# Seven products for 28 of the 32 hidden blocks of an MLP, and a last stage that goes token tile by token tile

## The chip, the cores and the metric

The kernel runs on one core of one Trainium2 chip. The metric is device time in microseconds for one execution of the whole decoder layer; several executions of a kernel are timed, one more is recorded by the profiler.

## The reference

One decoder layer on 512 tokens of width 1024, in float32. A token mixer (gated linear attention and latent attention, merged by gates) and an MLP each end in a residual sum and a layer norm:

```python
h = layer_norm(x, ln_in_g, ln_in_b)
...
mix = token_mixer(h, cos, sin, w_in[l], w_gla_a2[l], ...)
h = layer_norm(DEEPNORM_ALPHA * h + mix, ln1_g[l], ln1_b[l])
ff = jnp.square(jax.nn.relu(h @ w_ff1[l])) @ w_ff2[l]
h = layer_norm(DEEPNORM_ALPHA * h + ff, ln2_g[l], ln2_b[l])
```

The part that counts here is `ff`: `h` is 512 x 1024, `w_ff1` 1024 x 4096, `w_ff2` 4096 x 1024. The hidden width of 4096 is 32 blocks of 128.

## The kernel before

**Precision.** Every float32 operand of a large matmul is split into a high part (rounded to the matmul's format, on ACT) and a low part (the rest, on DVE): `split` at L104 for activations, L180 and L181 for weights. A product is then three matmuls: high x high, low x high, high x low.

**Weights.** `plan` appends the weight items to one list, `stream`, in the order in which the matmuls will use them. `pump(i)` (L152) runs ahead of item `i`: it issues loads on SP's queue into three `wraw` buffers, and splits the items that come next into `whi`/`wlo` (two buffers each), or into buffers of the general pool of 24 (`home` "a"), or back into `wraw` ("r"). Items whose source is already in SBUF carry `src` and `home` and no load.

**The MLP.** The loop over `ci` takes the hidden width in four chunks of eight blocks. In each, `gemm_fm` (L231 to L233) computes the first product with the hidden units on the partitions, and `ev_h` takes each block out of PSUM: relu, then square.

For chunks 0 to 2 the second product uses a scheme of seven products for a 2 x 2 by 2 x 2 block product (Winograd's form of Strassen's). The tokens are halved (0 to 255, 256 to 511), the hidden blocks are paired, the columns of `w_ff2` are halved. `win_hid` forms the sums of the hidden operand (tile `hx`), `win_sums` and a line of `win_f2` those of the weight quarters (tiles `T1`, `T2`, and in place T3 and T4); the quarters are loaded by `win_load` on POOL's queue (L1061). The table `WIN` gives the order: (weight operand, half of the chunk's blocks, product number). `win_f2` runs the products (L1116 to L1118), each in two PSUM banks of 128 tokens x 512 columns; some products add to the bank of an earlier one. When the second half of a product is done, ACT copies the bank to a buffer `ev` (L1128), and POOL issues DMAs that add it to the residual tiles `res` in SBUF (L1130), one DMA for each residual tile half that the product belongs to.

For chunk 3 the second product is an ordinary one: `ev_h` makes high and low parts of each hidden block (the square for the low part on POOL, L1159), and `gemm_tm` (L264 to L266) takes token tiles 0 and 1 together over all eight blocks, then tile 2; a loop written out (L1191 to L1193) takes tile 3, its second half in two strips of 256 columns, each with its own statistics. A tile's result is added to `res` on DVE (`ev_res`, L992, and L1195). `ln2` then aggregates the statistics, takes the power -1/2 on POOL (L1047), centres and scales on DVE (L1050, L1051) and writes the halves out on SP's queue (L1052).

**Order.** The program is traced in Python; a scheduler then sets a fixed order of instructions for each engine, by program order and a simulated time, and allots buffers. So an instruction whose operands are ready may stand ahead of earlier lines. Each engine and each queue then runs strictly in that order. PSUM has eight banks: four in the pool of `MM()`, four in that of `PX()`. The pool `pb` has 22 buffers (for `relu`, `ev`, and others), tag "C" has eight (four residual tiles, `T1`, `T2`, and the rows of gain and shift, `bc`).

Of the kernel before, what the change touches and what calls it, by code (L numbers as in the profile page):

```python
# [52 lines left out]
def tile_hybrid_block(ctx: ExitStack, tc: tile.TileContext, I, out, dbg=None):  # L53
# [259 lines left out]
    def plan_zip(key, specs):  # L313
        pls = [{"idx": [], "nk": 8, "per": 2} for _ in specs]
        for k0 in range(0, 8, 2):
# [12 lines left out]
           ("T4", 0, 4), ("T4", 1, 4), ("22", 0, 5), ("22", 1, 5), ("T3", 0, 6), ("T3", 1, 6))  # L328
    fb = 0
    for ci in range(FC):  # L330
        nb = 8
        for b, w in F1[ci]:
            PL["f1", ci, b] = plan("w_ff1", (fb + b) * P, w * P, res=(ci == 0 and b == 0), per=8 // w)
        if ci < FC - 1:
            PL["f2", ci] = []
            for n, (op, hf, _) in enumerate(WIN):
                PL["f2", ci].append(len(stream))
                stream.append({"src": lambda q=(ci, op, hf): WQ[q], "nk": 2, "n": T, "res": False,
                               "ahead": 2, "home": HOMES[n]})
        else:  # L340
            plan_zip("f2last", [("w_ff2", 0, fb, True), ("w_ff2", T, fb, True)])
        fb += nb
# [695 lines left out]
    def ln2(tt, bst=None):  # L1038
        mv = S([P, 2], F32, "mv")
        r = res[tt]  # L1040
        if bst is None:
            bst = S([P, 2, 6], F32, "bst")
            for j in range(2):
                nc.vector.bn_stats(bst[:, j, :], r[:, j * T:(j + 1) * T])
        nc.vector.bn_aggr(mv, bst)
        vts(mv[:, 1:2], mv[:, 1:2], LN_EPS, None, op0=ALU.add)
        gtt(mv[:, 1:2], mv[:, 1:2], mhalf[:, 0:1], op=ALU.pow)  # L1047
        for j in range(2):
            c = slice(j * T, (j + 1) * T)
            stt(r[:, c], r[:, c], mv[:, 0:1], bg[:, c], op0=ALU.subtract, op1=ALU.mult)  # L1050
            stt(r[:, c], r[:, c], mv[:, 1:2], bb[:, c], op0=ALU.mult, op1=ALU.add)  # L1051
            nc.sync.dma_start(out[tt * P:(tt + 1) * P, c], r[:, c])  # L1052
        yield

    def win_load(ci):
        w2 = I["w_ff2"].rearrange("(k p) n -> p k n", p=P)
        for op, i, j in (("12", 0, 1), ("11", 0, 0), ("22", 1, 1), ("21", 1, 0)):
            for hf in range(2):
# [5 lines left out]
    def win_sums(ci):  # L1064
# [5 lines left out]
        for hf in range(2):  # L1070
# [29 lines left out]
    def win_f2(ci, hid):  # L1100
        bank = {}
        for n, (op, hf, ph) in enumerate(WIN):
            i = PL["f2", ci][n]
            pump(i)
            hi, lo = stream[i]["w"]
            for pp in range(2):
                for t in range(2):
# [10 lines left out]
                    mm(o, xl[:, c], hi[:, pp], start=False, stop=hf == 1 and pp == 1, skip_group_check=True)  # L1118
                tick(4)
            if n in (5, 6):  # L1120
                t2, q21 = WT.pop((ci, n - 5))
                vtt(t2, t2, q21, op=ALU.subtract)
                WQ[ci, "T4", n - 5] = t2
            if hf == 1:
# [122 lines left out]
```

## Time and profile before

| | us |
|---|---|
| median of 3 runs | 903.77 |
| lowest, highest | 902.82, 903.8 |
| the profiled execution | 902.75 |
| its span, first to last instruction | 901.0 |

| busy, share of span | |
|---|---|
| PE (matmul) | 98% |
| DVE | 61% |
| ACT | 46% |
| POOL | 19% |

The profile is one execution recorded by hardware. In its rows L12 is line 12 of the kernel, `out<-in` names the tiles with their buffer numbers left out, `x16` is a count, and the time in brackets is idle time before an instruction with what ended it. PE is TensorE, PEld its weight loads, DVE VectorE, ACT ScalarE, POOL GpSimd, SP the engine whose queue issues most loads. A name with q (POOLq) is an engine's sequencer. A matmul's listed duration overlaps the next one's; from start to start is what it costs.

### The profile page before, as it was taken

What the parts mean: (1) busy time and instruction counts of PE and PEld (TensorE: products, weight loads), DVE (VectorE), ACT (ScalarE), POOL (GpSimd) and SP (SyncE); (2) the same over time, 40 slices, a digit from 0 to 9 for tenths busy, and PEclk for the clock granted to TensorE, in tenths of its full rate; (3) what the DMA queues carried; (4) which work ended last, traced back from release to release, by engine and by line L of the source; (5) the groups of instructions that cost most, each with busy time, mean ns of one, the idle gap of its engine ahead of it and who ended that gap; (6) DMA issues with size and microseconds to landing.
All of it is one profiled execution on the core that took longest, in us unless ns stands there. A gap on an engine that the chain in (4) does not pass through costs nothing.

```text
span 901.0 us, 11740 instructions
## 1 busy us (share of the span) xinstructions
PE 883.8 (98%) x4508; PEld 751.3 (83%) x4508; DVE 553.4 (61%) x905; ACT 412.7 (46%) x701; POOL 170.1 (19%) x192
## 2 busy tenths in 40 slices
PE   6999999999999999999999999999999999999996
PEld 5988888888888888888888888988888888888886
DVE  7835855575635244657756797997557646723576
ACT  6455443444434333435645423366357546643410
POOL 1003442442511010000000002104400520141201
PEclk9999999999999999999999999999999999999999
DMA  7413313212212332212207618005950990494312
GB/s 244 121 47 94 91 51 94 71 47 71 76 38 92 88 105 70 72 41 66 94 24 258 210 47 303 2 0 138 301 121 25 265 247 25 107 213 104 126 69 83
DMA packets 61159, 97.80 MB, mean 109 GB/s; under 512 B 7552, under 2 KB 27392, under 8 KB 61104
## 3 DMA queue, kind: packets, MB, share of 16 engines
q1 hardware_dynamic: 48816, 68.23, 23.9%
q0 software_dynamic: 10368, 25.17, 11.6%
q10 hardware_dynamic: 1920, 3.66, 1.2%
q8 instruction: 35, 0.57, 0.3%
q14 instruction: 20, 0.16, 0.1%
HBM read 82.36 MB, written 2.10 MB: 94 GB/s over the span
## 4 chain that ended last, share of the span: by engine, by line
PE 97%; ACT 1%; POOL 1%; DVE 1%; DMA 1%; issue 0%; SPq 0%; DVEq 0%
PE mm L231 16%; PE mm L233 15%; PE mm L232 15%; PE mm L264 7%; PE mm L266 7%; PE mm L265 7%; PE px L1116 2%; PE px L1118 2%; PE px L1117 2%; PE mm L1116 2%; PE mm L1118 2%; PE mm L1117 2%; PE px L679 2%; PE px L836 1%; PE px L366 1%; PE px L264 1%
## 5 line engine op out<-in xcount | busy, mean ns | idle before, releaser
L181 DVE TENSOR_TENSOR wlo<-wraw,whi 128x1024 fp32r<-128x1024 f32 (+1 forms) x104 | 117.7, 1133 | 169.6 <-ACT whi L180 162.2
L231 PE MATMUL mm<-h,whi 128*128 128x512 f32 x416 | 162.6, 392 | 0.4 <-ACT gt L923 0.4
L232 PE MATMUL mm<-h,whi 128*128 128x512 f32 x416 | 162.3, 390 | 0.0
L180 ACT ACTIVATE whi<-wraw 128x1024 fp32r<-128x1024 f32 (+1 forms) x104 | 100.3, 964 | 134.1 <-PE mm L232 82.4
L233 PE MATMUL mm<-h,wlo 128*128 128x512 f32 x416 | 154.4, 390 | 0.0
L231 PEld LDWEIGHTS mm<-h,whi 128*128 128x128 f32 x416 | 78.1, 188 | 16.3 <-ACT gt L923 0.6
L233 PEld LDWEIGHTS mm<-h,wlo 128*128 128x128 f32 x416 | 77.9, 188 | 16.4 <-DVE wlo L181 0.3
L232 PEld LDWEIGHTS mm<-h,whi 128*128 128x128 f32 x416 | 78.1, 188 | 15.7
L1130 POOL DMA_DIRECT2D res<-ev x48 | 42.2, 1042 | 188.9 <-ACT ev L1128 151.5
L265 PE MATMUL mm<-wlo,h 128*128 128x512 f32 x128 | 50.3, 393 | 0.0
L266 PE MATMUL mm<-whi,h 128*128 128x512 f32 x128 | 50.1, 392 | 0.0
L264 PE MATMUL mm<-whi,h 128*128 128x512 f32 x128 | 49.7, 403 | 0.0
L351 POOL TENSOR_TENSOR mv<-mv,mhalf 128x1 f32<-128x1 f32 x4 | 4.6, 1155 | 211.5 <-DVE mv L350 211.5
L180 ACT ACTIVATE xh<-wraw 128x1024 fp32r<-128x1024 f32 (+1 forms) x28 | 27.3, 986 | 34.8 <-PE mm L266 16.1
L618 POOL TENSOR_TENSOR rp<-rp 128x256 f32<-128x256 f32 x32 | 31.5, 984 | 60.8 <-ACT E L623 44.0
L1144 ACT ACTIVATE relu<-mm 128x512 f32<-128x512 f32 x32 | 18.8, 596 | 50.7 <-PE mm L233 50.6
L625 DVE TENSOR_TENSOR M<-E,qk 128x512 f32<-128x512 f32 x32 | 27.3, 854 | 16.5 <-ACT E L623 16.5
L181 DVE TENSOR_TENSOR xl<-wraw,xh 128x1024 fp32r<-128x1024 f32 (+1 forms) x28 | 31.1, 1126 | 8.0 <-ACT xh L180 8.0
L623 ACT ACTIVATE E<-rp 128x512 f32<-128x512 f32 x32 | 20.4, 638 | 26.9 <-POOL rp L619 26.9
L619 POOL TENSOR_TENSOR rp<-rp 128x256 f32<-128x256 f32 x32 | 27.6, 862 | 10.3 <-ACT q L648 8.1
L266 PEld LDWEIGHTS mm<-whi,h 128*128 128x128 f32 x128 | 24.1, 188 | 5.0
L265 PEld LDWEIGHTS mm<-wlo,h 128*128 128x128 f32 x128 | 24.1, 188 | 4.3
(369 smaller groups left out, 2196.1 us busy)
## 6 DMA issues: line engine op xcount, KB each, us to landing
wraw<-in_w_in_dram SPq DMA_DIRECT2D x40, 512.0 KB, 3.5
wraw<-in_w_ff_dram SPq DMA_DIRECT2D x40, 512.0 KB, 4.5
wq<-in_w_ff_dram POOLq DMA_DIRECT2D x24, 512.0 KB, 8.8
res<-ev POOLq DMA_DIRECT2D x48, 256.0 KB, 6.6
wraw<-in_w_o_gla_dram SPq DMA_DIRECT2D x8, 512.0 KB, 3.7
wraw<-in_w_o_mla_dram SPq DMA_DIRECT2D x8, 512.0 KB, 3.2
wraw<-in_w_out_dram SPq DMA_DIRECT2D x8, 512.0 KB, 4.0
wraw<-in_w_in_dram SPq DMA_DIRECT2D x8, 360.0 KB, 5.1
```

Of the source, the lines that this page charges most:

```text
L180: st["ins"] = act(hi[:, :nk, :n], raw[:, :nk, :n], AF.Copy)
L181: vtt(lo[:, :nk, :n], raw[:, :nk, :n], f(hi[:, :nk, :n]), op=ALU.subtract)
L231: mm(o, hi[:, c], xh, start=first, stop=False)
L232: mm(o, hi[:, c], xl, start=False, stop=False)
L233: mm(o, lo[:, c], xh, start=False, stop=last)
L264: mm(o, xh, hi[:, :n], start=opens, stop=False, skip_group_check=share)
L265: mm(o, xh, lo[:, :n], start=False, stop=False, skip_group_check=share)
L266: mm(o, xl, hi[:, :n], start=False, stop=last, skip_group_check=share)
L1116: mm(o, xh[:, c], hi[:, pp], start=opens, stop=False, skip_group_check=True)
L1117: mm(o, xh[:, c], lo[:, pp], start=False, stop=False, skip_group_check=True)
L1118: mm(o, xl[:, c], hi[:, pp], start=False, stop=hf == 1 and pp == 1, skip_group_check=True)
L1130: nc.gpsimd.dma_start(res[tt + t][:, j * T:(j + 1) * T], e, accum_op=ALU.add)
```

## The change

Chunk 3 uses the seven-product scheme for its first four blocks (one half in place of two: `HALVES`, `win_items`), with weight quarters loaded by `win_load(3)` on POOL's queue during chunk 2. Its last four blocks are an ordinary product, taken token tile by token tile. For tiles 2 and 3 ACT first copies the residual into the PSUM bank, and the matmuls add to it without a start flag; no add on DVE follows, and statistics and normalisation read PSUM. For tiles 0 to 2 the shift row is written to the output beforehand on SP's queue, ACT normalises, DVE multiplies by the gain, and a DMA on POOL's queue adds the tile to the output. Tile 3 is written as before. The evacuations of the seven products, L1128 and L1130, now occur in chunk 3 too.

```diff
@@ -326,19 +326,24 @@
     HOME = {"w": ("whi", "wlo"), "r": ("wraw", "wraw"), "a": ("xh", "xl")}
     WIN = (("11", 0, 0), ("21", 0, 1), ("11", 1, 0), ("21", 1, 1), ("T1", 0, 2), ("T1", 1, 2), ("T2", 0, 3), ("T2", 1, 3),
            ("T4", 0, 4), ("T4", 1, 4), ("22", 0, 5), ("22", 1, 5), ("T3", 0, 6), ("T3", 1, 6))
+
+    HALVES = (2, 2, 2, 1)
+
+    def win_items(ci):
+        return WIN if HALVES[ci] == 2 else [WIN[n] for n in (0, 1, 4, 6, 10, 8, 12)]
+
     fb = 0
     for ci in range(FC):
         nb = 8
         for b, w in F1[ci]:
             PL["f1", ci, b] = plan("w_ff1", (fb + b) * P, w * P, res=(ci == 0 and b == 0), per=8 // w)
-        if ci < FC - 1:
-            PL["f2", ci] = []
-            for n, (op, hf, _) in enumerate(WIN):
-                PL["f2", ci].append(len(stream))
-                stream.append({"src": lambda q=(ci, op, hf): WQ[q], "nk": 2, "n": T, "res": False,
-                               "ahead": 2, "home": HOMES[n]})
-        else:
-            plan_zip("f2last", [("w_ff2", 0, fb, True), ("w_ff2", T, fb, True)])
+        PL["f2", ci] = []
+        for n, (op, hf, _) in enumerate(win_items(ci)):
+            PL["f2", ci].append(len(stream))
+            stream.append({"src": lambda q=(ci, op, hf): WQ[q], "nk": 2, "n": T, "res": False,
+                           "ahead": 2, "home": (HOMES if ci < FC - 1 else "wwawawa")[n]})
+        if ci == FC - 1:
+            PL["f2last"] = [plan("w_ff2", j * T, T, fb + 4, fb + 8, res=True) for j in range(2)]
         fb += nb
 
 
@@ -1035,27 +1040,34 @@
             yield
 
 
-    def ln2(tt, bst=None):
-        mv = S([P, 2], F32, "mv")
-        r = res[tt]
-        if bst is None:
-            bst = S([P, 2, 6], F32, "bst")
+    def ln2(tt, bst, src):
+        mv, r = S([P, 2], F32, "mv"), res[tt]
+        rows = out[tt * P:(tt + 1) * P, :]
+        mean, var = mv[:, 0:1], mv[:, 1:2]
+        nc.vector.bn_aggr(mv, bst)
+        vts(var, var, LN_EPS, None, op0=ALU.add)
+        gtt(var, var, mhalf[:, 0:1], op=ALU.pow)
+        if tt < 3:
+
+            nmr = S([P, 1], F32, "nmr")
+            stt(nmr, mean, -1.0, var, op0=ALU.mult, op1=ALU.mult)
+            for c, p in src if tt > 1 else ((slice(0, D), r),):
+                act(r[:, c], p, AF.Identity, scale=var, bias=nmr)
+                vtt(r[:, c], r[:, c], bg[:, c], op=ALU.mult)
+            nc.gpsimd.dma_start(rows, r, accum_op=ALU.add)
+        else:
+            for c, p in src:
+                stt(r[:, c], p, mean, bg[:, c], op0=ALU.subtract, op1=ALU.mult)
             for j in range(2):
-                nc.vector.bn_stats(bst[:, j, :], r[:, j * T:(j + 1) * T])
-        nc.vector.bn_aggr(mv, bst)
-        vts(mv[:, 1:2], mv[:, 1:2], LN_EPS, None, op0=ALU.add)
-        gtt(mv[:, 1:2], mv[:, 1:2], mhalf[:, 0:1], op=ALU.pow)
-        for j in range(2):
-            c = slice(j * T, (j + 1) * T)
-            stt(r[:, c], r[:, c], mv[:, 0:1], bg[:, c], op0=ALU.subtract, op1=ALU.mult)
-            stt(r[:, c], r[:, c], mv[:, 1:2], bb[:, c], op0=ALU.mult, op1=ALU.add)
-            nc.sync.dma_start(out[tt * P:(tt + 1) * P, c], r[:, c])
+                c = slice(j * T, (j + 1) * T)
+                stt(r[:, c], r[:, c], var, bb[:, c], op0=ALU.mult, op1=ALU.add)
+                nc.sync.dma_start(rows[:, c], r[:, c])
         yield
 
     def win_load(ci):
         w2 = I["w_ff2"].rearrange("(k p) n -> p k n", p=P)
         for op, i, j in (("12", 0, 1), ("11", 0, 0), ("22", 1, 1), ("21", 1, 0)):
-            for hf in range(2):
+            for hf in range(HALVES[ci]):
                 t = A([P, 2, T], F32, "wq")
                 k0 = 8 * ci + 4 * hf + i
                 nc.gpsimd.dma_start(t, w2[:, k0:k0 + 3:2, j * T:(j + 1) * T])
@@ -1067,7 +1079,7 @@
                 if "ev" in st:
                     gates.enter_context(tc.issue_after(st["ev"].ins))
                 vtt(*a, **kw)
-        for hf in range(2):
+        for hf in range(HALVES[ci]):
             q12 = WQ.pop((ci, "12", hf))
             t1 = WQ[ci, "T1", hf] = A([P, 2, T], F32, "T1")
             held(t1, q12, WQ[ci, "11", hf], op=ALU.subtract)
@@ -1099,9 +1111,10 @@
 
     def win_f2(ci, hid):
         bank = {}
-        for n, (op, hf, ph) in enumerate(WIN):
+        nh = HALVES[ci]
+        for n, (op, hf, ph) in enumerate(win_items(ci)):
             i = PL["f2", ci][n]
-            pump(i)
+            pump(i + max(0, n - 3) if nh == 1 else i)
             hi, lo = stream[i]["w"]
             for pp in range(2):
                 for t in range(2):
@@ -1115,34 +1128,35 @@
                     xh, xl = hid[2 * hf + pp][ph]
                     mm(o, xh[:, c], hi[:, pp], start=opens, stop=False, skip_group_check=True)
                     mm(o, xh[:, c], lo[:, pp], start=False, stop=False, skip_group_check=True)
-                    mm(o, xl[:, c], hi[:, pp], start=False, stop=hf == 1 and pp == 1, skip_group_check=True)
+                    mm(o, xl[:, c], hi[:, pp], start=False, stop=hf == nh - 1 and pp == 1, skip_group_check=True)
                 tick(4)
-            if n in (5, 6):
-                t2, q21 = WT.pop((ci, n - 5))
+            if n in ((5, 6) if nh == 2 else (2,)):
+                h = n - 5 if nh == 2 else 0
+                t2, q21 = WT.pop((ci, h))
                 vtt(t2, t2, q21, op=ALU.subtract)
-                WQ[ci, "T4", n - 5] = t2
-            if hf == 1:
+                WQ[ci, "T4", h] = t2
+            if hf == nh - 1:
                 for t in range(2):
                     o = bank[{3: 0, 6: 0, 5: 2}.get(ph, ph), t]
                     e = B([P, T], F32, "ev")
                     st["ev"] = act(e, o, AF.Copy, scale=-1.0 if ph == 4 else 1.0)
                     for tt, j in (((0, 0),), ((0, 0),), ((2, 1),), ((0, 1),), ((2, 0),), ((0, 1),), ((2, 0), (2, 1)))[ph]:
                         nc.gpsimd.dma_start(res[tt + t][:, j * T:(j + 1) * T], e, accum_op=ALU.add)
-            if n == 9 and ci + 1 < FC - 1:
+            if n == 9 and ci + 1 < FC:
                 win_load(ci + 1)
 
     WQ, WT = {}, {}
     for ci in range(FC):
         nb = 8
         hid = []
-        win = ci < FC - 1
+        last = ci == FC - 1
         if ci == 0:
             win_load(0)
 
         def ev_h(a, ps):
             r = B([P, T], F32, "relu")
             act(r, ps, AF.Relu)
-            if win:
+            if len(hid) <= 2 * HALVES[ci] - (a % 2 == 0):
                 if a % 2 == 0:
                     hid.append({"R": A([P, 2, T], F32, "hr")})
                 ops = hid[-1]
@@ -1165,37 +1179,43 @@
                 t_r1 = spawn(residual1())
             else:
                 gemm_fm(PL["f1", ci, b], h1T, w * P, ev_h, width=2)
-            if win and b == 0:
+            if b == 0:
                 t_ws = spawn(win_sums(ci))
         if ci == 0:
             finish(t_r1)
-        if win:
-            finish(t_ws)
-            for hf in range(2):
-                WT[ci, hf] = (WQ[ci, "T2", hf], WQ[ci, "21", hf])
-            win_f2(ci, hid)
-        else:
+        finish(t_ws)
+        for hf in range(HALVES[ci]):
+            WT[ci, hf] = (WQ[ci, "T2", hf], WQ[ci, "21", hf])
+        win_f2(ci, hid)
+        if last:
+            hid = hid[2:]
             bg, bb = bcast_row("ln2_g"), bcast_row("ln2_b")
-            gemm_tm(PL["f2last"], hid, T, ev_res, tts=(0, 1))
-            spawn(ln2(0))
-            spawn(ln2(1))
-            gemm_tm(PL["f2last"], hid, T, ev_res, tts=(2,))
-            spawn(ln2(2))
-            tt, r, bst = 3, res[3], S([P, 4, 6], F32, "bst4")
-            for c0, n in ((0, T), (T, 256), (T + 256, 256)):
-                acc = MM()[:, :n]
-                ws = slice(c0 % T, c0 % T + n)
-                for k in range(nb):
-                    hi, lo = weights(PL["f2last"][c0 // T], k)
-                    xh, xl = hid[k][:, 0, tt * P:], hid[k][:, 1, tt * P:]
-                    mm(acc, xh, hi[:, ws], start=k == 0, stop=False)
-                    mm(acc, xh, lo[:, ws], start=False, stop=False)
-                    mm(acc, xl, hi[:, ws], start=False, stop=k == nb - 1)
-                    tick(None)
-                vtt(r[:, c0:c0 + n], acc, r[:, c0:c0 + n], op=ALU.add)
-                for j in range(c0 // 256, (c0 + n) // 256):
-                    nc.vector.bn_stats(bst[:, j, :], r[:, j * 256:(j + 1) * 256])
-            finish(spawn(ln2(3, bst)))
+            for tt in range(3):
+                nc.sync.dma_start(out[tt * P:(tt + 1) * P, :], bb)
+            for tt in range(NT):
+                r, bst = res[tt], S([P, 4, 6], F32, "bst4")
+
+                src, on = [], tt > 1
+                for c0, n in ((0, T), (T, T)) if tt < 3 else ((0, T), (T, 256), (T + 256, 256)):
+                    acc = (PX if tt == 2 else MM)()[:, :n]
+                    if on:
+                        act(acc, r[:, c0:c0 + n], AF.Copy)
+                    ws = slice(c0 % T, c0 % T + n)
+                    for k in range(4):
+                        hi, lo = weights(PL["f2last"][c0 // T], k)
+                        xh, xl = [hid[k][:, i, tt * P:(tt + 1) * P] for i in range(2)]
+                        mm(acc, xh, hi[:, ws], start=k == 0 and not on, stop=False, skip_group_check=on)
+                        mm(acc, xh, lo[:, ws], start=False, stop=False, skip_group_check=on)
+                        mm(acc, xl, hi[:, ws], start=False, stop=k == 3, skip_group_check=on)
+                        tick(None)
+                    if not on:
+                        vtt(r[:, c0:c0 + n], acc, r[:, c0:c0 + n], op=ALU.add)
+                        acc = r[:, c0:c0 + n]
+                    src.append((slice(c0, c0 + n), acc))
+                    for j in range(n // 256):
+                        nc.vector.bn_stats(bst[:, c0 // 256 + j, :], acc[:, j * 256:(j + 1) * 256])
+                t = spawn(ln2(tt, bst, src))
+            finish(t)
 
 
 # ---- launch ----
```

## The prediction

> **What bounds the kernel now.** I read the page's busy table and chain first, then the stages in windows, then single instructions of the last stage.
>
> ```profile
> span 901.0 us, 11740 instructions
> PE 883.8 (98%) x4508; PEld 751.3 (83%) x4508; DVE 553.4 (61%) x905; ACT 412.7 (46%) x701; POOL 170.1 (19%) x192
> PE 97%; ACT 1%; POOL 1%; DVE 1%; DMA 1%; issue 0%; SPq 0%; DVEq 0%
> ...
> 768.30:806.50 38.20, 38.20 (x170) 31.63 (x169) 22.38 (x23) 23.54 (x33) 10.41 (x12) 1.00 0.73 165
> 806.50:850.10 43.60, 43.60 (x194) 36.12 (x193) 14.64 (x12) 15.06 (x22) 8.76 (x9) 1.00 0.47 133
> 850.10:872.00 21.90, 21.90 (x98) 18.12 (x98) 14.17 (x14) 8.33 (x11) 5.13 (x4) 1.00 0.21 73
> 872.00:888.00 16.00, 16.00 (x73) 13.23 (x71) 13.91 (x27) 0.00 (x0) 2.98 (x3) 1.00 0.18 68
> 888.00:894.00 6.00, 5.91 (x49) 5.70 (x47) 2.35 (x6) 0.00 (x0) 0.00 (x0) 1.00 0.22 83
> 894.00:901.00 7.00, 0.00 (x0) 0.00 (x0) 3.86 (x8) 0.00 (x0) 0.99 (x1) 0.75 0.20 75
> ```
>
> TensorE makes 97% of the chain. The windows (columns: length, then busy time and count of PE, weight load, DVE, ACT, POOL, then granted clock, DMA share, GB/s) are chunk 2's seven products, chunk 3's first product, its second product in three pieces, and the tail. PE is full in all but the last, so two things shorten the time: fewer matmuls, or a shorter tail after the last one. Anything else counts only if it makes PE wait. The rows that give the price of a matmul:
>
> ```profile
> 849.92 0.39 PE L264 MATMUL mm<-xh,hid 128*128 128x512 f32 x1
> ...
> 888.00 0.28 PE L1191 MATMUL mm<-xh,hid 128*128 128x256 f32 x1
> ...
> 893.63 0.28 PE L1193 MATMUL mm<-xh,hid 128*128 128x256 f32 x1
> ```
>
> The second product starts at 849.92. Up to 888.00 it has 3 x 48 + 24 = 168 matmuls of 512 columns (token tiles 0 to 2, and the first half of tile 3): 38.08/168 = 0.2267 us each, start to start. Then 48 of 256 columns start between 888.00 and 893.63: 5.63/47 = 0.120 us each.
>
> **TensorE's share of the change.** Seven products over four hidden blocks are 7 x 2 x 2 x 3 = 84 matmuls of 512. The other four blocks cost 24 per token tile: 72 for tiles 0 to 2, and 12 of 512 plus 24 of 256 for tile 3. That is 84 + 72 + 12 = 168 of 512, as many as before, and 24 of 256 instead of 48. Removed: 24 x 0.120 = 2.88 us. If nothing waits, products end at 849.9 + 84 x 0.2267 = 868.9, tile 0 at 874.4, tile 1 at 879.8, tile 2 at 885.3, tile 3 at 890.9.
>
> **The tail.**
>
> ```profile
> 893.95 0.42 DVE L1195 TENSOR_TENSOR res<-mm,res 128x256 f32<-128x256 f32 x1 [1.99 <-PE mm L1193]
> 894.41 0.43 DVE L1197 BATCH_NORM_STATS2 bst<-res 128x6 f32<-128x256 f32 x1
> 894.87 0.26 DVE L1045 BATCH_NORM_AGGREGATE mv<-bst 128x2 f32<-128x24 f32 x1
> 895.16 0.15 DVE L1046 TENSOR_SCALAR mv<-mv 128x1 f32<-128x1 f32 x1
> 895.24 1.40 DVE L1050 SCALAR_TENSOR_TENSOR res<-res,mv,bc 128x512 f32<-128x512 f32 x2
> 896.56 1.41 DVE L1051 SCALAR_TENSOR_TENSOR res<-res,mv,bc 128x512 f32<-128x512 f32 x2
> ...
> 895.40 0.99 POOL L1047 TENSOR_TENSOR mv<-mv,mhalf 128x1 f32<-128x1 f32 x1 [9.26 <-DVE mv L1046]
> ...
> DMA to landing us min/median/max: 2.0/2.0/2.0
> ```
>
> With the residual already in PSUM the add of L1195 goes: statistics start 894.41 - 893.95 = 0.46 us sooner after the last matmul. No row here has statistics or a two-scalar operation that reads PSUM. The add at L1195 does read it and takes 0.42 us, as its statistics on SBUF take 0.43, so I take equal durations (bounds: 0.1 us either way). The centring is cut in three (512, 256, 256) in place of two: two pieces of 0.42 for one of 0.70 (1.40/2) is 0.14 us more; I take 0.15 (bounds 0 to 0.3, at the lower end because POOL's power, running until 896.39, covers nearly all of the two pieces). The tail thus shortens by 0.46 - 0.15 = 0.31 us. The output write of tile 3 (the row of 2.0 us to landing, the two writes after 897) stays as it is.
>
> The normalisation of tiles 0 to 2 moves partly to ACT, idle from 872 to 888 in the window above. For DVE a tile of rows 0 or 1 is two adds, four statistics, an aggregate and one multiply of 1024:
>
> ```profile
> L992 DVE TENSOR_TENSOR res<-mm,res 128x512 f32<-128x512 f32 x6 | 4.1, 686 | 5.7 <-PE mm L266 5.7
> L1197 DVE BATCH_NORM_STATS2 bst<-res 128x6 f32<-128x256 f32 x4 | 1.6, 423 | 0.1
> L1160 DVE TENSOR_TENSOR hid<-relu,hid 128x512 fp32r<-128x512 f32 x4 | 5.2, 1313 | 8.1 <-POOL relu L1159 8.1
> L181 DVE TENSOR_TENSOR xl<-wraw,xh 128x1024 fp32r<-128x1024 f32 x6 | 7.2, 1216 | 2.8 <-ACT xh L180 2.8
> ```
>
> 2 x 0.69 + 4 x 0.42 + 1.22 + about 0.6 of small ones = 4.9 us, under the 5.4 us that PE spends on a tile. So it is hidden; without that cover it would cost the part above 5.4. The three writes of the shift row to the output go out long before they matter: the shift row depends only on a free buffer, and PE shows no idle time even in stages where the DMA share is 0.73 (first window). I cost them at nothing; if the cover were gone, the price is a weight load that comes late, the next rival but one.
>
> **Moved into chunk 3's first product.** Four quarter loads join POOL's queue in chunk 2, where chunks 0 and 1 have eight each; three sums and a T4 of 1.22 and two pairs' operands join DVE, which is busy 14.6 of 43.6 us there (second window). The waits of PE over the whole span say what such work has cost so far:
>
> ```profile
> PE px L366 <- ACT x L355: 8.8, 1, 8.8
> PE mm L233 <- DVE wlo L181: 0.5, 1, 0.5
> ```
>
> The first is the start of the kernel, the second the longest since. So I take nothing; uncovered, one sum of 1.22 us that comes late costs at most itself.
>
> **The sum.** 901.0 - 2.88 - 0.31 = 897.8 us of span. I add 0.2 us for a wait somewhere in the new products (below): 898.0. The profiled execution took 902.75 us in all, 1.75 around its span: 899.8. The three runs have their median at 903.77, 1.0 above that execution, so the change of -3.0 us gives 900.8 for the median.
>
> **What could make PE wait.** The residual is what is new: tile 2's matmuls may start only when ACT has copied its residual to PSUM, and that needs the last products' accumulating writes to have landed in it. These go out on POOL's queue, in order, two per product (four for the seventh), and a write to the same residual half waits for the one before it.
>
> ```profile
> L1130 POOL DMA_DIRECT2D res<-ev x30 | 26.4, 1046 | 80.9 <-ACT ev L1128 56.3 <-DMA res<-ev 15.9 <-DMA wq<-in_w_ff_dram 5.4
> ...
> DMA to landing us min/median/max: 3.3/6.6/14.5
> ...
> res<-ev POOLq DMA_DIRECT2D x16, 256.0 KB, 4.7
> ...
> 806.81 3.51 POOL L1130 DMA_DIRECT2D res<-ev  x4 [3.70 <-ACT ev L1128]
> ```
>
> Issue takes 3.51/4 = 0.87 us. In the order of the new chunk (11, 21, T1, T2, 22, T4, T3) three neighbours hit the same half: 11 then 21, T2 then 22, T4 then T3. Products now end every 12 x 0.2267 = 2.72 us, half the distance of earlier chunks. I lay the queue out with a landing time L. First write at 853.3 (product 11 ends at 852.6, evacuation 0.6); 21's pair at 853.3 + L; four issues until T2's first write; one L until 22's; two issues until T4's; one L until T3's, and one until that has landed: 853.3 + 4L + 6 x 0.87, and 0.4 for the steps between, so 858.9 + 4L. With L = 4.3 that is 876.1, with 4.9 it is 878.5, with 6.6 it is 885.3. Tile 2's copy (as long as an evacuation, 0.6, and a step) must start by 879.8 - 0.7 = 879.1. The point from which PE waits is thus L = 5.05. The median over all chunks is 6.6 us, but that holds the stages in which the 512 KB quarter loads share the queue (the row with 14.5 at its far end); over chunk 2's last stretch the sixteen writes have 4.7 us, and the new chunk has no such loads after it. I take 4.5 us and a wait of nothing to 0.5 us.
>
> [...]
>
> **Weights.** Seven splits instead of none, then four instead of eight: 11 splits against 8, each 1.06 on ACT and 1.22 on DVE, plus 14 evacuations of 0.6 on ACT.
>
> ```profile
> 848.08 1.28 ACT L1144 ACTIVATE relu<-mm 128x512 f32<-128x512 f32 x2 [6.31 <-PE mm L233]
> ...
> 850.77 1.06 ACT L180 ACTIVATE xh<-wraw 128x1024 fp32r<-128x1024 f32 x1
> ...
> 852.20 1.16 ACT L1158 ACTIVATE hid<-relu 128x512 fp32r<-128x512 f32 x2
> ...
> L1128 ACT ACTIVATE ev<-px 128x512 f32<-128x512 f32 x7 | 4.1, 598 | 6.3 <-DMA res<-ev 5.1 <-PE px L1118 1.0
> ```
>
> The second product's weights share a pair of buffers with the first product's last item, free at 849.9. Split at once they are ready at 849.9 + 1.06 + 1.23 = 852.2, before the first product ends at 852.6. Behind all four relus and squares, which end on ACT at 852.2 + 1.16 = 853.4, they come at 855.7 less overlap: 3 us late, unless PE takes the third product first. I take 0.1 to 0.2, because PE was full through the same passage of chunk 2 (first window).
>
> **The rivals.**
>
> *The residual comes late (slower).* One mechanism: accumulating writes that wait for each other on POOL's queue, in front of tile 2's copies. It decides from L = 5.05, or from L = 4.5 if POOL's four squarings of relu (L1159, up to 1.6 us each where DVE reads beside it) push the first write by over 2 us. At L = 6.6 tile 2 starts at 886.0 instead of 879.8: a wait of 6.2 us, so 6.2 - 3.2 = +3.0 and 906.8 us. For it: POOL's 15.9 us of waits for such landings in the rows above. Against it: 4.7 us in the last stretch. The last window shows a granted clock of 0.75 once PE has stopped. [...]
>
> *The end moves to tile 2's output (no change or small gain).* Its 512 KB accumulating write into DRAM is issued near 890.2 (tile 2 ends 885.3; statistics, power 1.0, ACT and multiply). No row shows such a write. Nearest: 3.3 us for 256 KB alone, and this for 512 KB:
>
> ```profile
> wq<-in_w_ff_dram POOLq DMA_DIRECT2D x24, 512.0 KB, 8.8
> ```
>
> It lands between 893.5 and 899.0. Tile 3's last write lands near 897.97 - 3.19 + 2.0 = 896.8. Above 6.6 us it sets the end, at 8.8 by 2.2 us: gain 1.0, 902.8 us. I take 5.5 us (256 KB alone, plus as much again for bytes), hidden.
>
> *Weights or evacuations late at the seam.* ACT would have 4.2 us of relu and squares, at most 10 splits and 14 evacuations before 869: 4.2 + 10.6 + 8.4 = 23.2 us in 21, if none is brought forward. Late by 1.5 to 2 us, it leaves a gain of 1.2 to 1.7: 902.3 us. Against it: splits are seen ahead of their use everywhere, and PE never waited.
>
> **Chances.** The forecast, a gain of 2 to 3.4 us, 0.60; the late residual 0.17 (0.13 of it a loss of over 1.8 us); tile 2's output 0.10; the seam 0.13. A measurement of this kernel tells about 0.2% from no change, 1.8 us. The forecast is faster, with a third of the seam: 0.64. The slower end is the late residual and mishaps of the others' far ends: 0.19. The rest, 0.17, lies within. The range goes from 899.1 (no wait, and a tail better by 0.5, seen from the lowest run, 902.82, with 3.7 off) to 905.3 (late residual at L = 6.2: a wait of 4.6 us). The likeliest case alone: 900.2 to 901.8.
>
> **What would show it.** Right: 512-column matmuls counting 168 after the first product of chunk 3 ends and 24 of 256 columns; no PE idle time before tile 2; last matmul near 890.9; the aggregate 0.46 us closer to it. Wrong: PE idle with a release by ACT's copy, which itself waited for a residual write (late residual); the chain ending in a POOL write to the output (tile 2); PE idle ended by a split or an evacuation between 850 and 869 (the seam).

## The result: half a per cent slower, and the profile after

| us | before | after |
|---|---|---|
| median (6 runs each) | 903.18 | 908.34 |
| lowest, highest | 902.82, 903.8 | 907.72, 909.42 |
| span of the profiled execution | 901.0 | 905.7 |

The ratio is 1.0057, with an interval of 1.0044 to 1.0070: slower by 5.2 us on the median, a small loss but clear of the noise. The forecast was 900.8 us, the range 899.1 to 905.3; the time lies above both. The profiled execution is among the fastest of the six (907.72 us); the spans of the others run up to 1.7 us longer, and no profile shows why. The page of the changed kernel (span; busy time; chain by engine) shows that the arithmetic did go away:

```profile
span 905.7 us, 11763 instructions
PE 881.6 (97%) x4484; PEld 747.8 (83%) x4484; DVE 558.3 (62%) x919; ACT 432.1 (48%) x733; POOL 181.6 (20%) x211
PE 91%; DMA 2%; DVE 2%; ACT 2%; POOL 1%; issue 1%; SPq 0%; DVEq 0%; POOLq 0%; ACTq 0%
```

There are 4508 - 4484 = 24 matmuls fewer, as counted beforehand. But TensorE's share of the chain fell from 97% to 91%: other work now sets the time at the end. The timeline of TensorE (start, duration; in brackets the idle time before and its releaser) gives the borders of the new stages. The first row opens the seven products, the second tile 0, the third tile 2, the last ends the matmuls:

```profile
849.97 0.61 PE L1129 MATMUL px<-whi,h1p 128*128 128x512 f32 x2
...
869.78 0.39 PE L1207 MATMUL mm<-xh,hid 128*128 128x512 f32 x1
...
883.81 0.50 PE L1207 MATMUL px<-xh,hid 128*128 128x512 f32 x1 [2.99 <-ACT px L1202]
...
894.85 0.28 PE L1209 MATMUL mm<-xh,hid 128*128 128x256 f32 x1
```

With the rows of before, the 4.7 us of span can be laid out along TensorE, in us:

| | |
|---|---|
| 24 matmuls fewer, 24 x 0.120 | -2.9 |
| seven products take 869.78 - 849.97 = 19.81 instead of 84 x 0.2267 = 19.04 | +0.8 |
| TensorE waits for ACT's copy of tile 2's residual | +3.0 |
| later start and single steps | +0.3 |
| *last matmul: 894.85 instead of 893.63* | *+1.2* |
| last matmul to the last aggregate: 2.76 instead of 1.24 | +1.5 |
| aggregate to the end of DVE: 3.30 instead of 3.10 | +0.2 |
| end of DVE to the end of the span: 4.8 instead of 3.0 | +1.8 |
| *tail: 10.85 instead of 7.37* | *+3.5* |

**The wait.** The windows of the changed kernel (length; busy time of PE, weight load, DVE, ACT, POOL; granted clock, DMA share, GB/s) around tiles 0 and 1 and the wait:

```profile
855.30:869.00 13.70, 13.69 (x60) 10.85 (x59) 12.68 (x11) 11.64 (x18) 7.97 (x9) 1.00 0.87 146
869.00:874.50 5.50, 5.50 (x26) 4.56 (x25) 1.22 (x2) 2.04 (x3) 3.51 (x4) 1.00 0.97 203
874.50:880.00 5.50, 5.50 (x26) 4.53 (x26) 4.71 (x13) 0.00 (x0) 4.07 (x5) 1.00 1.09 183
880.00:885.30 5.30, 2.31 (x10) 1.59 (x9) 0.69 (x1) 1.96 (x4) 0.00 (x0) 1.00 0.69 118
```

From 869 to 880 the DMA share is 0.97 and 1.09 (the time of all packets over sixteen engines, so packets that overlap take it above 1): the DMA engines are full, at about 190 GB/s. At that rate one write of 256 KB takes an estimated 0.262 MB / 190 GB/s = 1.4 us of all of them, while POOL issues one every 0.88 (3.51/4 in the rows below). ACT and POOL show who stands in that queue (timelines of the changed kernel, POOL first):

```profile
855.23 1.76 POOL L1144 DMA_DIRECT2D res<-ev  x2
...
864.02 1.74 POOL L1144 DMA_DIRECT2D res<-ev  x2 [0.76 <-ACT ev L1142]
870.41 3.51 POOL L1144 DMA_DIRECT2D res<-ev  x4 [4.65 <-DMA res<-ev]
875.02 3.51 POOL L1144 DMA_DIRECT2D res<-ev  x4 [1.11 <-ACT ev L1142]
```

```profile
872.19 1.06 ACT L180 ACTIVATE xh<-wraw 128x1024 fp32r<-128x1024 f32 x1 [4.12 <-DMA wraw<-in_w_ff_dram]
873.15 1.07 ACT L1142 ACTIVATE ev<-px 128x512 f32<-128x512 f32 x2
883.15 1.12 ACT L1202 ACTIVATE px<-res 128x512 f32<-128x512 f32 x2 [8.93 <-DMA res<-ev]
884.46 1.21 ACT L1202 ACTIVATE mm<-res 128x512 f32<-128x512 f32 x3 [0.18 <-DMA res<-ev]
885.61 1.23 ACT L1055 ACTIVATE res<-res,nmr,mv 128x1024 f32<-128x1024 f32 x1
```

The copies of the residual (L1202) start at 883.15. The four writes issued from 875.02 on land at 880.6, 881.8, 883.1 and 884.4, and by the trace's semaphores the copy that TensorE waits for is released by the third of them. T3's writes to the first column halves, which T4's writes hit too, are issued behind those to the second halves; so the half of tile 2 that is used first lands 2.5 us after its other half. All five copies stand ahead of the normalisation of tile 0 (L1055), which is ready at 879.8 and starts at 885.61.

**The tail.** DVE's last work in the changed kernel (timeline), and the issues of DMAs in its last 50 us (size, median us to landing):

```profile
895.05 0.42 DVE L1216 BATCH_NORM_STATS2 bst<-mm 128x6 f32<-128x256 f32 x1
896.07 0.69 DVE L1056 TENSOR_TENSOR res<-res,bc 128x512 f32<-128x512 f32 x1 [0.58 <-ACT res L1055]
896.67 0.42 DVE L1216 BATCH_NORM_STATS2 bst<-mm 128x6 f32<-128x256 f32 x1
897.01 0.68 DVE L1056 TENSOR_TENSOR res<-res,bc 128x512 f32<-128x512 f32 x1
897.61 0.26 DVE L1047 BATCH_NORM_AGGREGATE mv<-bst 128x2 f32<-128x24 f32 x1
...
899.50 1.41 DVE L1063 SCALAR_TENSOR_TENSOR res<-res,mv,bc 128x512 f32<-128x512 f32 x2
```

```profile
res<-ev POOLq DMA_DIRECT2D x16, 256.0 KB, 5.4
out_dram<-res POOLq DMA_DIRECT2D x3, 512.0 KB, 5.1
wraw<-in_w_ff_dram SPq DMA_DIRECT2D x1, 512.0 KB, 6.6
out_dram<-res SPq DMA_DIRECT2D x2, 256.0 KB, 3.5
```

The multiplies of tile 2 (L1056) stand on DVE in front of tile 3's last statistics and in front of its aggregate, and wait for ACT. Tile 2's output, issued at 897.99, is still being added to DRAM when tile 3's two writes start: these land after 3.5 us, where before they took 2.0.

**The chain.** The table counts along TensorE, but the chain of work that ended last (start, duration) leaves TensorE in the seven products and does not come back to it:

```profile
877.04 7.31 DMA res<-ev
...
884.99 0.68 ACT mm L1202 x2
885.67 1.18 ACT res L1055
886.87 1.23 DVE res L1056
...
890.67 1.25 ACT res L1055
891.94 1.23 DVE res L1056
...
895.25 0.79 ACT res L1055
896.07 0.69 DVE res L1056
```

The last write to the residual lands, ACT makes its copies, and then tiles 0, 1 and 2 are normalised one behind the other, 5.1 and 4.6 us apart. TensorE needs 5.4 us for a tile, so a normalisation that begins 5.8 us late is still late at the end. In this execution the late residual thus reaches the end through ACT, and TensorE's wait of 3.0 us runs beside that chain.

### The profile page after: what moved, and what is told of

It reads as the page before. It is cut to its first block, busy times and chain, and to the rows that moved or that the text cites. A ratio compares the mean times of both kernels' runs of the same rounds, so it can differ in the third digit from the quotient of the medians.

```text
span 905.7 us, 11763 instructions
## 1 busy us (share of the span) xinstructions
PE 881.6 (97%) x4484; PEld 747.8 (83%) x4484; DVE 558.3 (62%) x919; ACT 432.1 (48%) x733; POOL 181.6 (20%) x211
## 4 chain that ended last, share of the span: by engine, by line
PE 91%; DMA 2%; DVE 2%; ACT 2%; POOL 1%; issue 1%; SPq 0%; DVEq 0%; POOLq 0%; ACTq 0%
PE mm L231 15%; PE mm L233 15%; PE mm L232 15%; PE mm L264 6%; PE mm L266 6%; PE mm L265 6%; PE px L1130 3%; PE px L1131 2%; PE px L1129 2%; PE mm L1130 2%; PE mm L1131 2%; PE mm L1129 2%; PE px L684 2%; DMA res<-ev 1%; PE px L841 1%
## 5 line engine op out<-in xcount | busy, mean ns | idle before, releaser
L1144 POOL DMA_DIRECT2D res<-ev x64 | 55.9, 1027 | 195.9 <-ACT ev L1142 148.7
L180 ACT ACTIVATE xh<-wraw 128x1024 fp32r<-128x1024 f32 (+1 forms) x24 | 23.2, 979 | 28.7 <-PE mm L266 16.2
L181 DVE TENSOR_TENSOR xl<-wraw,xh 128x1024 fp32r<-128x1024 f32 (+1 forms) x24 | 26.4, 1112 | 9.1 <-ACT xh L180 8.9
L181 DVE TENSOR_TENSOR wlo<-wq,whi 128x1024 fp32r<-128x1024 f32 x14 | 18.0, 1283 | 20.7 <-ACT whi L180 20.7
```

What stands on the lines that cost most here:

```text
L180: st["ins"] = act(hi[:, :nk, :n], raw[:, :nk, :n], AF.Copy)
L181: vtt(lo[:, :nk, :n], raw[:, :nk, :n], f(hi[:, :nk, :n]), op=ALU.subtract)
L1144: nc.gpsimd.dma_start(res[tt + t][:, j * T:(j + 1) * T], e, accum_op=ALU.add)
```

## The experiments

The theory was two causes that do not depend on each other. R: sixteen accumulating writes fill the DMA engines, so the residual comes late. N: the way of normalising tiles 0 to 2 (ACT, DVE, POOL's output DMA) is longer than what TensorE spends on a tile, and so reaches into the tail. (The recorded expectations call N theory O.) The chain above shows already that in the changed kernel the two meet: R's late writes start N's chain. The rival of N is that the tail is late only because the wait was. The rival of R is the order: writes to the same half that wait for each other, or evacuations behind a weight split.

**No residual in PSUM.**

```diff
-                src, on = [], tt > 1
+                src, on = [], False
```

> No residual is copied into PSUM; tiles 2 and 3 are added on DVE after their matmuls, as tiles 0 and 1. Theory R (the residual's accumulating writes land late; PE waits 3.0 us for tile 2's copy, and the five copies hold ACT, so that tile 0's normalisation starts at 885.6 and the work piles up into the tail): PE's wait at tile 2 goes, tile 0's normalisation starts before 882, the span falls from 905.7 by 3 to 5 us, to 901 to 903. Theory O (tile 2's own route, over ACT and an accumulating output write, lengthens the tail whenever it runs): the 3.0 us go, the tail from last matmul to end stays at 10 to 11 us: 903 or more.

904.52 us, ratio 1.0014 [1.0005, 1.0024]. TensorE waits nowhere in this stage and ends at 891.90. The tail (DVE, timeline) shows the same pattern as the changed kernel:

```profile
892.55 0.68 DVE L1056 TENSOR_TENSOR res<-res,bc 128x512 f32<-128x512 f32 x1
893.15 0.42 DVE L1216 BATCH_NORM_STATS2 bst<-res 128x6 f32<-128x256 f32 x1
893.49 0.68 DVE L1056 TENSOR_TENSOR res<-res,bc 128x512 f32<-128x512 f32 x1
894.08 0.26 DVE L1047 BATCH_NORM_AGGREGATE mv<-bst 128x2 f32<-128x24 f32 x1
```

From the last matmul to the end of the span it is 902.5 - 891.90 = 10.6 us, against 7.37 before. The span lies where theory R put it (901 to 903), the tail where theory O did. So the long tail is there without the wait: N holds, its rival falls, and without the wait the change is still no gain. Against the kernel before, the 3.2 us more are 0.9 to the last aggregate, with tile 2's two multiplies (0.6 each from start to start) in front of it, 0.2 to the end of DVE, and 2.0 behind it, where tile 3's writes take 3.7 us beside tile 2's output.

**Tile 2 normalised like tile 3**, on DVE, with writes on SP's queue; the copies stay.

```diff
-        if tt < 3:
+        if tt < 2:
...
-            for c, p in src if tt > 1 else ((slice(0, D), r),):
+            for c, p in ((slice(0, D), r),):
...
-            for tt in range(3):
+            for tt in range(2):
                 nc.sync.dma_start(out[tt * P:(tt + 1) * P, :], bb)
```

> Tile 2 is normalised on DVE and written on SP's queue as tile 3 is; the copies into PSUM stay. Theory R: PE's wait of 3.0 us stays, and tiles 0 and 1 are still late on ACT; the span falls by 0.5 to 2 us only, to 904 to 905. Theory O: the tail falls back to 7.4 us or so, the span to about 902.3.

907.03 us, ratio 1.0042 [1.0027, 1.0057]. The tail falls to 904.9 - 897.39 = 7.5 us, close to the old 7.37. That flatters tile 2's new path, because the last matmul itself came late, which gave DVE time; without a wait the same path has a tail of 9.35 us (below). A wait of 3.3 us stays, and another price appears: the window after it has a granted clock of 0.64.

```profile
885.30:890.00 4.70, 4.70 (x15) 3.69 (x14) 2.23 (x5) 2.38 (x4) 0.74 (x1) 0.64 0.00 0
```

The last matmul is 897.39 - 894.85 = 2.5 us later than in the changed kernel. Of this 0.6 is a later start of the stage (POOL's first squaring at 850.58 instead of 850.01) and 0.3 the longer wait. From the start of the copy that ends the wait (884.05) to the last matmul it is 897.39 - 884.05 = 13.34 us instead of 894.85 - 883.15 = 11.70: 1.6 us with the clock lower.

**Fewer neighbours that hit the same half.** In this kernel products 21 and T2 of chunk 3 are added to the other column half of the residual, so that one pair of neighbours is left instead of three.

```diff
+                    to1, to3 = ((0, 0), (0, 1)) if nh == 2 else ((0, 1), (0, 0))
-                    for tt, j in (((0, 0),), ((0, 0),), ((2, 1),), ((0, 1),), ...
+                    for tt, j in (((0, 0),), (to1,), ((2, 1),), (to3,), ...
```

> In chunk 3 products 21 and T2 are added to the other column half of the residual (so the output is not the reference's), which leaves one pair of neighbouring writes to the same half in place of three; number and size of the writes are the same. Rival C (landings that wait for each other): the last write of tile 2 lands 4 to 6 us sooner than 883.1, PE does not wait, the span is 902 or 903. Theory R with DMA engines as the limit (sixteen writes at about 1.4 us each from 855 on): it lands within 1.5 us of 883.1, PE waits 1.5 to 3 us, the span stays within 1.5 us of 905.7.

906.71 us in one execution. The copy starts at 882.06 instead of 883.15 and TensorE waits 1.6 us instead of 3.0: this order is worth 1.1 us of the copy's start and 1.4 us of the wait, not all of it.

**The seventh product without DMA writes.** DVE adds T3 from PSUM; 12 accumulating writes instead of 16.

```diff
+                    if nh == 1 and ph == 6:
+                        for j in range(2):
+                            rj = res[2 + t][:, j * T:(j + 1) * T]
+                            vtt(rj, o, rj, op=ALU.add)
+                        continue
                     e = B([P, T], F32, "ev")
```

> The seventh product of chunk 3 is added to the residual by DVE from PSUM (four adds of 0.69 us) instead of by four accumulating DMAs: twelve writes in place of sixteen. Theory R: tile 2's copy can start near 879, PE waits less than 0.7 us, ACT is free by 881, the span falls to 900 to 902. Theory O: PE's wait goes, the tail stays 10 to 11 us: 902.5 to 903.5.

905.63 us, ratio 1.0025 [1.0016, 1.0035]. No wait; the copies start at 876.27, and the last matmul at 891.67. The windows (the last two columns are DMA share and GB/s) show the DMA engines run dry in the very stretch in which the changed kernel waited:

```profile
874.50:880.00 5.50, 5.50 (x26) 4.57 (x25) 4.41 (x9) 1.80 (x3) 0.00 (x0) 1.00 0.65 111
880.00:885.30 5.30, 5.30 (x26) 4.37 (x25) 4.51 (x12) 2.02 (x3) 0.56 (x1) 1.00 0.00 0
```

A quarter of the writes less, and the copy is 6.9 us earlier. The last write lands at 879.3 instead of 884.4: 5 us for four writes, 1.3 us each, close to the 1.4 from the rate. The tail is 903.7 - 891.67 = 12.0 us, in a second kernel without a wait, and the span lies a little above the 902.5 to 903.5 of theory O. Not all of the tail is N's: DVE's four adds wait for writes to land and stand in front of tile 0's statistics, so that tile 0's normalisation starts on ACT only at 882.87.

**The evacuations first.** The split of the last weight item, which kept ACT waiting 4.12 us, is placed behind T3's two evacuations.

```diff
+            if st["spl"] == st.get("hold"):
+                break
...
+            if nh == 1 and n == 6:
+                st["hold"] = len(stream) - 1
...
+        if ci == FC - 1:
+            del st["hold"]
+            st["gates"] = (st["ev"],)
```

> As the changed kernel, but the split of the last weight item of the ordinary product is placed behind the two evacuations of the seventh product on ACT (there it waited 4.1 us for its load, with the evacuations behind it). If that is what made the residual late: the seventh product's writes are issued from 871 or 872 on instead of 875, tile 2's copy starts near 880, PE waits under 0.5 us. If the writes before them on POOL's queue, or the DMA engines, are the limit: the last four are issued at about 874, 1.1 us sooner, tile 2's copy starts near 882, PE waits about 2 us.

907.08 us, ratio 1.0042 [1.0028, 1.0055]. The evacuations are earlier (868.62 and 869.98 instead of 873.15 and 873.63), the copy hardly: 882.78, a wait of 2.6 us. Here and in the next kernel the granted clock behind the wait was lower as well, 0.79 and 0.83 from 885.3 to 890.0 (last section).

**Both orders at once**, with products 21 and T2 again added to the other half.

> The edits of e3 and e5 together (the output is not the reference's: products 21 and T2 of chunk 3 are added to the other column half). Neither neighbouring writes to one half nor ACT now holds the seventh product's writes. If the DMA engines are the limit (sixteen writes at 1.4 us each and a load of 512 KB, from 855 on), tile 2's copy still starts at 880 or later. If the two holds together were the whole of it, the last four writes go out from 871 on and the copy starts at 877 to 878, and PE does not wait.

906.73 us in one execution, a wait of 2.2 us. The split is out of the way, and of the neighbours only T4 and T3 are left, whose writes hit the same first halves. The windows, POOL's issue of the write that the copy waits for, and the copy read:

```profile
869.00:874.50 5.50, 5.50 (x26) 4.55 (x25) 0.58 (x1) 2.24 (x3) 2.71 (x4) 1.00 1.11 239
874.50:880.00 5.50, 5.50 (x26) 4.57 (x25) 4.45 (x9) 0.00 (x0) 1.12 (x2) 1.00 1.12 199
```

```profile
876.85 0.86 POOL L1149 DMA_DIRECT2D res<-ev  x1 [4.24 <-DMA res<-ev]
...
882.75 1.12 ACT L1210 ACTIVATE px<-res 128x512 f32<-128x512 f32 x2 [8.86 <-DMA res<-ev]
```

The share is 1.11 and 1.12, and the copy starts within 1.1 us of the changed kernel's in all three kernels with another order. The last of the sixteen writes lands at 883.3, 884.0 and 884.0 in them, against 884.4: none of the three orders made the sixteen land sooner by more than 1.1 us, while four writes fewer did by 5. R holds for the time at which all have landed, and so for the chain through ACT.

TensorE's wait is another matter, for it hangs on one write. POOL stood 4.24 us for T4's write before it could issue this one, and in the changed kernel the second half of tile 2 landed at 880.6, 2.5 us before the first. An order in which tile 2 takes its second half first was not tried. By the rows of the changed kernel it would let the copy start near 880.6, and a matmul follows 0.66 us behind the copy's start (883.81 - 883.15), so an estimate of the wait is 0.4 us instead of 3.0. The chain through tile 3's copies would stay.

**Both causes away**: no copies, and tile 2 like tile 3 (the first two edits together).

> The edits of e1 and e2 together: no copy into PSUM, and tile 2 goes the way of tile 3. If the two losses add up (PE's wait and ACT held; tile 2's route in the tail): last matmul near 891.9 as in e1, tail of 7.5 to 8 us as in e2: span 899.5 to 900, 1 to 1.5 us under the kernel before. If DVE's added work (two adds for each of tiles 2 and 3) takes the tail over: span 901 to 902, no gain.

903.38 us, ratio 1.0002 [0.9993, 1.0011]: no change. The span of 901.3 is not the 899.5 to 900 of two losses that add up, but the 901 to 902 of the other branch. No wait; tail 901.3 - 891.95 = 9.35 us. Against the kernel with no copies alone, whose last matmul starts at 891.90, only tile 2's path differs: it is worth 10.6 - 9.35 = 1.25 us of the tail. The windows show a new bound, DVE (third column of busy times), full for eight microseconds:

```profile
890.00:894.00 4.00, 2.23 (x19) 2.02 (x17) 4.00 (x10) 0.00 (x0) 0.93 (x1) 1.00 0.83 132
894.00:898.00 4.00, 0.00 (x0) 0.00 (x0) 3.93 (x10) 0.00 (x0) 0.92 (x1) 0.85 0.35 131
```

**A copy for tile 3 alone**, placed behind tile 0's normalisation on ACT; tile 2 like tile 3, the evacuations first. It takes tile 3's adds from DVE, at a time when the residual has landed.

```diff
-                src, on = [], tt > 1
+                src, on = [], tt > 2
...
-                        act(acc, r[:, c0:c0 + n], AF.Copy)
+                        with tc.issue_after(st["id"].ins):
+                            act(acc, r[:, c0:c0 + n], AF.Copy)
```

> The edits of e2 and e5, and the copy into PSUM for tile 3 alone, placed behind tile 0's normalisation on ACT. The residual of tile 3 has landed by 884, its matmuls start at 886, so PE does not wait; ACT holds nobody; the tail loses one add. Expected: last matmul near 891.9, tail 7.4 us, span 899.0 to 899.6, about 1.5 to 2 us under the kernel before. If DVE is the limit in the tail: 900 to 901.

902.09 us, ratio 0.9988 [0.9979, 0.9997]: the best of all, 6.3 us under the changed kernel and about 1.1 under the kernel before, still not the 899.0 to 899.6 expected. No wait; tail 900.2 - 892.08 = 8.1 us. What is left of N (DVE, timeline): tile 2's last pair of multiplies and adds, L1067, still stands in front of tile 3's last statistics.

```profile
891.92 1.40 DVE L1067 SCALAR_TENSOR_TENSOR res<-res,mv,bc 128x512 f32<-128x512 f32 x2
893.24 0.42 DVE L1226 BATCH_NORM_STATS2 bst<-mm 128x6 f32<-128x256 f32 x1
893.70 0.26 DVE L1049 BATCH_NORM_AGGREGATE mv<-bst 128x2 f32<-128x24 f32 x1
```

**The squares on DVE**, to see whether POOL's four squarings cause the 0.8 us in the seven products; added to the kernel above.

```diff
-            gtt(r, r, r, op=ALU.mult)
+            vtt(r, r, r, op=ALU.mult)
```

> As e8, with the four squarings of relu in chunk 3 on DVE in place of POOL. In e8 DVE's operations beside them took up to 2.1 us instead of 1.2, and the seven products 19.8 us instead of 19.04. If POOL's squarings are the reason: products in 19.3 us or less, first accumulating write before 855, span 0.4 to 0.8 us under e8's 900.2. If DVE's four more operations (0.7 us each) hold the splits as much: no change, 900.0 to 900.5.

902.29 us, ratio 0.9988 [0.9979, 0.9997]: no gain over the kernel above. From the first of the seven products to the last matmul it is 892.23 - 850.42 = 41.81 us. Of this 0.7 is a new wait of TensorE for ACT's copy of tile 3's residual, and 41.1 are left, against 892.08 - 850.47 = 41.61 in the kernel above. So some 0.5 us of the seam did come back, and the copy took it: it stands behind tile 0's normalisation, which starts on ACT at 884.83 instead of 882.39.

**Tile 2's second half in PSUM too**, added to that kernel.

```diff
-                src, on = [], tt > 2
...
+                    on = tt > 2 or (tt == 2 and c0 == T)
```

> As e9, and tile 2's second half also takes its residual in PSUM (its write lands near 880, its matmuls start at 883), which takes an add of 0.69 us from DVE. If DVE's work after 880 sets the tail: 0.4 to 0.7 us under e9. If its copy comes late: a wait of PE of about 1 us and no gain.

902.49 us, ratio 0.9990 [0.9981, 0.9999]: no gain either. The last matmul starts at 892.71, the end is at 901.2: the tail is 8.5 us instead of 8.3, and the wait of 0.7 for tile 3's copy stays. DVE does end 0.4 us sooner after the last matmul (4.45 us instead of 4.84), but from there to the end it is 4.0 us instead of 3.4. POOL issues tile 1's output later, at 891.55 instead of 889.96; whether that is the cause is not shown.

## Why the prediction was wrong, point by point

Counted along TensorE, the span came out 7.7 us above the forecast's 898.0: 3.8 in the tail, 2.8 in the wait (3.0 where 0.2 was added), 0.8 in the seam and 0.3 in single steps.

*TensorE's share: right.* 24 matmuls fewer, no idle time in tiles 0 and 1 (the windows from 869 to 880 are full). The stretch predicted for everything, 890.9 - 849.9 = 41.0 us, was measured without its wait in the kernel with the squares on DVE: 41.1.

*The landing time: the step that failed first.* "I take 4.5 us and a wait of nothing to 0.5 us." The median was 5.4, beyond the turning point of 5.05, and the wait 3.0 us. The layout of the queue came close: with the first write at 855.23 (and not 853.3, since POOL's squarings stood in front of it), its formula gives 860.8 + 4 x 5.4 = 882.4 for a copy that came at 883.15. Part of that is luck: the writes took from 3.3 to 7.4 us, and T3's went out when ACT had evacuated its product, behind the split that waited for its load, not when T4's had landed. What was wrong was to treat the landing time as a property of one write. It grew with the queue already in the prediction's own burst, the four writes from 806.81: the first pair landed in 4.6 us, the last in 6.5 (medians). In the kernel before, the window of that burst, and its DMAs issued in 806.8 to 807.6 and in 809.4 to 810.4 (two issues are counted in each):

```profile
806.80:813.00 6.20, 6.20 (x29) 5.11 (x29) 0.10 (x1) 1.46 (x2) 3.51 (x4) 1.00 0.98 211
```

```profile
res<-ev POOLq DMA_DIRECT2D x2, 256.0 KB, 4.6
...
res<-ev POOLq DMA_DIRECT2D x2, 256.0 KB, 6.5
```

Four writes and a weight load filled the engines (share 0.98), and the time to landing rose through the four. The sum to make was of bytes: sixteen writes and one weight load of 512 KB are 4.72 MB. At the 211 GB/s of that window they take 22.4 us: from 853.3, where the prediction had the first write, to 875.7, and from 855.23 to 877.6, against the 879.1 at which the copy had to start. By itself this sum would not have forecast a wait. But it leaves only 3.4 or 1.5 us for everything that runs below that rate, and the engines moved 146 GB/s from 855.3 to 869 and 183 from 874.5 to 880.

*The rival "the residual comes late"* had the mechanism, the place and the turning point, and its formula, wait less 3.2, would have made 3.0 - 3.2, about nothing. So TensorE's wait alone does not explain a loss. The rival named the wait of TensorE as the price, and not the copies that hold ACT, through which the late residual reached the end.

*The tail: the largest error.* "The tail thus shortens by 0.31 us" became 3.5 us longer. The add was saved as described, but "so it is hidden" compared DVE's 4.9 us of work per tile with TensorE's 5.4. The normalisation is a chain over three engines: aggregate, POOL's power (in the changed kernel behind the issue of the previous output, 0.89), one small step on DVE, ACT 1.24, and the multiply. For tile 2 without any wait before it (no residual in PSUM) it ran from the aggregate at 889.14 to the end of the second multiply at 894.17, while TensorE had finished at 891.90. What of tile 2 stood on DVE ahead of tile 3's last pieces, two multiplies of 0.68 there, was added to the tail. In the changed kernel this chain starts from the late copies on ACT. How its 10.85 us would divide between the two is not shown: the kernels without a wait had other work on DVE.

*Tile 2's output.* Its landing, 5.1 us, was close to the 5.5 taken, and it was not what ended last. But it was not free: tile 3's writes behind it took 3.5 us. Without tile 2's output on that queue the end of DVE to the end of the span is 3.3 us (kernel with both causes away) instead of 4.8 to 5.1.

*The seam* lost 0.8 us where 0.1 to 0.2 was taken; its rival had 1.5 to 2. Two of DVE's splits took 2.06 and 2.26 us beside POOL's squarings, against 1.22 without (below); with the squares on DVE some 0.5 us came back.

**What stays open.** The best kernel has a tail of 8.1 us where 7.06 was forecast, and its gain of 1.15 us is little more than a third of the forecast's 3.0. An order of DVE that puts tile 3's statistics ahead of tile 2's last pair was not tried, nor was T3 added by DVE in the best kernel, nor another order of tile 2's halves. The best kernel lies only 0.1% under the kernel before, and its two variants are no different from it.

## What to carry to other kernels

Before latencies are chained, divide the bytes of a burst by the rate of an earlier full window: here a median landing time of 4.7 us, measured in a looser queue, was 5.4 us with sixteen writes in a row. A sum that leaves little room is a warning. Ask also which of the transfers the next step needs first, and what else stands behind that step on its engine. When the last tile's work is split over several engines, compare the length of its chain, not each engine's busy time, with the time that covers it; an instruction of the tile before that stands ahead of the last tile's on its engine can be paid for in full once the last matmul is done (here tile 2's path was worth 1.25 us of the tail). And keep large writes away from the last few microseconds: here the final writes took 3.5 us behind a write of 512 KB that landed before them, and 2.0 us in the kernel before.

## What the runs showed of the hardware that was not expected

TensorE waited for ACT's copy of tile 2's residual in five kernels. In three of them its granted clock was lower behind the wait, in two it was not (us; the clocks are means over a window; the last column runs from the start of the copy to the last matmul):

| kernel | wait | clock, 880.0 to 885.3 | clock, 885.3 to 890.0 | copy to last matmul |
|---|---|---|---|---|
| products to the other half | 1.6 | 1.00 | 1.00 | 893.75 - 882.06 = 11.69 |
| both orders | 2.2 | 0.83 | 0.83 | 896.04 - 882.75 = 13.29 |
| evacuations first | 2.6 | 0.86 | 0.79 | 896.07 - 882.78 = 13.29 |
| the changed kernel | 2.99 | 1.00 | 1.00 | 894.85 - 883.15 = 11.70 |
| tile 2 like tile 3 | 3.3 | 1.00 | 0.64 | 897.39 - 884.05 = 13.34 |

With the clock lower, the way from the copy to the last matmul took 1.6 us more. The length of the wait alone does not tell the three from the two: the changed kernel kept its clock through 2.99 us, the kernel with both orders did not through 2.2. What decides it is not shown by these five executions, one of each kernel.

Some of DVE's splits took longer while POOL was squaring. Two of them in the changed kernel (timeline), the first beside a squaring on POOL (1.33 us from 853.96), the second without one:

```profile
854.31 2.06 DVE L181 TENSOR_TENSOR wlo<-wq,whi 128x1024 fp32r<-128x1024 f32 x1
...
863.20 1.22 DVE L181 TENSOR_TENSOR wlo<-T,whi 128x1024 fp32r<-128x1024 f32 x1
```

A third, from 856.89 beside a squaring of 1.68 us from 856.38, took 2.26. With the squares on DVE its busy time from 849.9 to 869.0 was 4.85 + 11.87 = 16.72 us with the four squarings in it, against 3.72 + 13.18 = 16.90 without them in the kernel that this one changes.
